# Where token rows begin in SBUF: high rows at 32, low rows at 160 modulo 256 bytes, and eight idle matmuls instead of fourteen

## The chip, the cores and the metric

The kernel runs on one core of one Trainium2 chip. The metric is the device time of one execution in microseconds (us); lower is better. Before the change it is 1536.18 us, the median of three runs that lie between 1535.31 and 1536.74 us.

## What is computed

The reference is one step of a decoder layer in which three head groups work side by side. It takes a new sequence of 4096 tokens and 64 sample tokens (8 sequences of 8), each a row of 1024 numbers:

```
h = rmsnorm(x, g_pre)
z = h @ w_in                      # 1024 -> 2816 columns
cb, cc, ch, cg, q, k, v, ag, mq, mg = split_cols(z)
out_a = silu(cg) * cb * conv3(cc * ch)            # 256 columns
out_b = silu(ag) * window_attention(q, k, v, sink)  # 512 columns, window 128
out_c = silu(mg) * attention(mq, memory)          # 256 columns, 256 memory tokens
y = concat(out_a, out_b, out_c) @ w_out
x = x + rmsnorm(y, g_post)
```

All data are float32. The outputs are the new x for all tokens and the new caches of keys, values and convolution inputs. The change concerns the product `h @ w_in`, the first and longest part of the kernel.

## The kernel before, in words

**Number format.** TensorE is fed in the type float32r. The kernel splits each operand in two: a high part, which is the number as copied into that type, and a low part, which is the rest. A product is then the sum of three matmuls: high weights with high tokens, high weights with low tokens, low weights with high tokens. `product` (lines 362 to 369, the matmul at line 368) does this for one 128-column group of weights and 260 tokens: 4 steps over the inner dimension, 3 matmuls each, 12 in all, accumulated in one PSUM bank.

**Products.** The 4160 tokens are cut into 8 blocks of 520, two halves of 260 each. The 22 groups of 128 columns of `w_in` are taken in pairs. For the blocks from the third on in phase 0, and for all blocks in phases 1 and 2, the 2 x 2 block product of a pair of column groups is made with seven products instead of eight (`PRODUCTS`, a Strassen-like scheme with sums such as S1 to S4 of the weights and T1 to T4 of the tokens). The first two blocks of phase 0 (`plain_block`) use the ordinary eight. Phases 0 and 1 treat four pairs, phase 2 three. So the loops over phase, block, product, pair, inner step and high/low issue all matmuls of line 368, in program order.

**Order of the work.** While the products of one step run, the parts for the next step are made: `split` (line 355) writes the high part with ScalarE (line 358) and the low part with VectorE (line 359); `x_split` (line 577) does the same for the first two blocks, with the gain of the norm folded in. Loading, scaling, sums, eviction of PSUM by VectorE (line 375) or ScalarE (line 377) and the finishing of each column group are issued between the products in an order written out by hand. PE takes its matmuls in that order and waits for a part only if it is late.

**Where the operands lie.** A token tile is `[128, 4, 320]` float32: per partition four rows, one for each inner step, each padded from 260 to 320 numbers. 320 numbers are 1280 bytes, five times 256, so all four rows begin at the same place modulo 256 bytes. The tiles come from the pool `hp`, two under the tag "hi" and two under "lo". A pool named `shift` with one tile of 32 numbers (128 bytes per partition) is opened just ahead of `hp` (line 92); nothing uses the tile, it only moves `hp` and every pool that is opened behind it on that side. The weight tiles are `[128, 2, 512]`, high and low, in the pools `wa` and `wb`; each weight load takes 128 numbers, 512 bytes. Weights and tokens of line 368 all begin at 224 modulo 256.

**The opening.** TensorE first runs fourteen matmuls on a tile of ones (`warm`, line 701 to 704) whose result is thrown away. Meanwhile the first tokens and weights arrive and are split; the first real product follows.

**Behind the input projection** come the attention chunks and the output projection (line 1494, 512 columns a matmul, and attention lines such as 1184, 1248, 1199 and 1271). They begin when the pools of the input projection are closed, and open pools of their own in that place. Line 791 multiplies the memory tokens by their weights, between products of phase 2.

Of the kernel before, what the change touches and what calls it, by code (L numbers as in the profile page):

```python
# [8 lines left out]
F32 = mybir.dt.float32  # L9
F32R = mybir.dt.float32r  # L10
# [5 lines left out]
P = 128  # L16
D = 1024
KT = D // P
KH = KT // 2
# [4 lines left out]
HW = 260  # L24
XR = 320
# [22 lines left out]
def f(ap):  # L48
    return ap.bitcast(F32)
# [3 lines left out]
def hybrid_layer(ctx: ExitStack, tc: tile.TileContext, a: dict):  # L53
# [31 lines left out]
    pa = ExitStack()  # L85
# [3 lines left out]

    place = ctx.enter_context(tc.tile_pool(name="place", bufs=1)).tile([P, 2, KH, HW], F32, name="place")  # L90
    hxp = pa.enter_context(tc.tile_pool(name="hx", bufs=4))
    pa.enter_context(tc.tile_pool(name="shift", bufs=1)).tile([P, 32], F32, name="shift")
    hp = pa.enter_context(tc.tile_pool(name="hp", bufs=2))
    own = ExitStack()
    kept_z = ExitStack()
# [66 lines left out]
    def store(dst, src):  # L162
        if store_queue[0] is G:
            G.dma_start(dst, src)
        else:
            late.append(lambda: DMA.dma_start(dst, src))
# [153 lines left out]
    def gain_of(o, k):  # L320
        kk = KH * (int(o[1]) - 1) + k
        return gpre[:, kk : kk + 1]
# [16 lines left out]
    def t_sum(ph, b, o):  # L339
# [9 lines left out]
        if ph == 1:  # L349
# [2 lines left out]
                tc.keep_in_program_order(ins)  # L352
            store(hd[b][o], ops[o])

    def split(src, name):
        hi = hp.tile([P, KH, XR], F32R, tag="hi", name=f"hi{name}")[:, :, :HW]
        lo = hp.tile([P, KH, XR], F32R, tag="lo", name=f"lo{name}")[:, :, :HW]
        S.copy(hi, src)
        V.tensor_tensor(lo, src, f(hi), op=ALU.subtract)
        return hi, lo  # L360
# [157 lines left out]
    def h_split(i):  # L518
        if i < len(steps):
            ph, b, p = steps[i]  # L520
            o = PRODUCTS[p][1]
            hs[i] = split(xs[ph, b][o], f"{ph}_{b}{o}")
# [52 lines left out]
    raw0, zz, pending, h0, kept = {}, {}, {}, {}, {}  # L575

    def x_split(b, o, meanwhile=lambda: None):
        x = xs[0, b][o]
        h0[b, o] = hi, lo = [hp.tile([P, KH, XR], F32R, tag=n, name=f"{n}0_{b}{o}")[:, :, :HW] for n in ("hi", "lo")]
        for k in range(KH):  # L580
            if k == 1:
                meanwhile()
            g = gain_of(o, k)
            S.mul(hi[:, k], x[:, k], g)
            V.scalar_tensor_tensor(lo[:, k], x[:, k], g, f(hi[:, k]), op0=ALU.mult, op1=ALU.subtract)
# [37 lines left out]
    def plain_jobs(b, s):  # L623

        gains = lambda b, *os: [lambda o=o: x_gain(0, b, o) for o in os]
        scales = lambda b, *os: [lambda o=o: x_scale(0, b, o) for o in os]
        parts = lambda b, o: [lambda: x_split(b, o)]
        fill = lambda o: [lambda q=q: first_fill(o, q) for q in range(4)]
        sums = lambda q, k: [lambda: first_sums(q, k)]
# [70 lines left out]
    idle = accumulator(1, 2, "idle")  # L700
    warm = hp.tile([P, KH, XR], F32R, tag="lo", name="warm").rearrange("p k n -> p (k n)")
    G.memset(f(warm[:, : P + 512]), 1.0)
    for n in (416, 416, 416, 416, 512, 512, 512, 416, 416, 416, 260, 260, 260, 260):
        TE.matmul(idle[:, 0, :n], warm[:, :P], warm[:, P : P + n], start=True, stop=True)  # L704
    x_split(0, "B11", lambda: first_fill("A21", 0))
    for q in range(4):
        if q > 0:
# [743 lines left out]
    class Block:  # L1451
# [10 lines left out]
        def split(self):  # L1462
# [13 lines left out]
            self.hl = [hi, lo]  # L1476

        def run(self, last, start, split, starts):
            b, m = self.b, self.m
            yn = work([P, D], "yn", f"yn{b}")  # L1480
# [4 lines left out]
            for p, (c0, c1) in enumerate(parts):  # L1485
                if p == 1:
                    split()
                acc = psum("z", f"y{b}_{p}")[:, : c1 - c0]
                j, passes = 0, 3 if m == P else 2
                for k in range(KT):  # L1490
                    if k in starts:
                        start()
                    for l, r in ((0, 0), (1, 0), (0, 1)) if m == P else ((0, 0), (0, 1)):
                        TE.matmul(acc, self.hl[l][:, k], wo[k][c0 // 512][:, r, c0 % 512 : c0 % 512 + c1 - c0], start=j == 0, stop=j == passes * KT - 1)  # L1494
                        j += 1
                if m < P:
                    S.copy(yn[:m, c0:c1], acc[m : 2 * m])
                    V.tensor_tensor(acc[:m], acc[:m], yn[:m, c0:c1], op=ALU.add)
                end = last and p == 2
                if not end:  # L1500
                    V.tensor_tensor(yn[:m, c0:c1], acc[:m], gpost[:m, c0:c1], op=ALU.mult)  # L1501
                S.activation((psum("t", "sq") if end else acc)[:m, : c1 - c0], acc[:m], AF.Square, scale=float(D) ** -0.5, accum_out=st[:m, p : p + 1])  # L1502
                if last and p == 1:
                    V.tensor_tensor(st[:m, 0:1], st[:m, 0:1], st[:m, 1:2], op=ALU.add)
# [180 lines left out]
```

## Time and profile before

| what | value |
|---|---|
| median of three runs | 1536.18 us |
| the profiled execution, device time | 1533.46 us |
| its span, first to last instruction | 1531.7 us |
| TensorE granted clock, mean | 0.999 |
| PE (matmul) busy | 1520.7 us, 99% of the span |
| PEld (weight load) busy | 1398.8 us, 91% |
| VectorE (DVE) busy | 1145.3 us, 75% |
| ScalarE (ACT) busy | 806.1 us, 53% |
| GpSimd (POOL) busy | 380.0 us, 25% |

The engines run side by side, so the busy times add up to more than the span. A busy row of PE or PEld counts the time from the start of an instruction to its modelled end; matmuls are pipelined, so each row overlaps the next, and the distance between two starts is shorter than the duration of one. The trace calls a token part `hi_` or `lo_` with a digit and a letter of the operand, a weight tile `w_`, the PSUM bank `c`. In a row of a group, the last figure ahead of the bar is the count, then come busy time in us and the mean duration in ns; in a row of one line's view, the three figures are the shortest, the median and the longest duration in ns, then the first and the last start. A row of a window gives its bounds in us and its length, the busy time of each engine with the number of instructions in it, the granted clock, the busy share of the DMA engines and GB/s. A row of the timeline or of the chain begins with start and length in us.

### The profile page before, as it was taken

What the parts mean: (1) busy time and instruction counts of PE and PEld (TensorE: products, weight loads), DVE (VectorE), ACT (ScalarE), POOL (GpSimd) and SP (SyncE); (2) the same over time, 40 slices, a digit from 0 to 9 for tenths busy, and PEclk for the clock granted to TensorE, in tenths of its full rate; (3) what the DMA queues carried; (4) which work ended last, traced back from release to release, by engine and by line L of the source; (5) the groups of instructions that cost most, each with busy time, mean ns of one, the idle gap of its engine ahead of it and who ended that gap; (6) DMA issues with size and microseconds to landing.
All of it is one profiled execution on the core that took longest, in us unless ns stands there. A gap on an engine that the chain in (4) does not pass through costs nothing.

```text
span 1531.7 us, 30162 instructions
## 1 busy us (share of the span) xinstructions
PE 1520.7 (99%) x11337; PEld 1398.8 (91%) x11337; DVE 1145.3 (75%) x2055; ACT 806.1 (53%) x2039; POOL 380.0 (25%) x604
## 2 busy tenths in 40 slices
PE   9999999999999999999999999999999999999998
PEld 9999999999999999999999998788888888888876
DVE  6789888898978777897777679766666666666743
ACT  6786566476222222354454447755665565565632
POOL 0223332221400000000101204544444444444310
PEclk9999999999999999999999999999999999999999
DMA  9989999878755333677877789977777777776332
GB/s 257 199 225 246 274 283 267 277 244 284 194 181 181 127 126 127 225 231 278 229 272 227 230 291 260 239 151 159 148 148 151 155 156 150 160 161 146 131 110 96
DMA packets 177942, 306.28 MB, mean 200 GB/s; under 512 B 33925, under 2 KB 107653, under 8 KB 177765
## 3 DMA queue, kind: packets, MB, share of 16 engines
q1 hardware_dynamic: 130901, 227.38, 48.2%
q0 software_dynamic: 46176, 75.92, 25.1%
q8 instruction: 90, 1.47, 0.4%
q10 hardware_dynamic: 720, 1.05, 0.2%
q14 instruction: 55, 0.45, 0.1%
HBM read 197.23 MB, written 108.05 MB: 199 GB/s over the span
## 4 chain that ended last, share of the span: by engine, by line
PE 93%; DVE 3%; DMA 1%; ACT 1%; issue 1%; POOL 0%; SPq 0%; DVEq 0%; POOLq 0%; ACTq 0%
PE c L368 53%; PE y L1494 23%; PE ws L1248 4%; PE wo L1090 2%; PE wt L1271 2%; PE xs L1184 2%; PE xt L1199 2%; PE wo L1220 2%; PE wo L1226 1%; PE mem_acc L791 1%; DMA nat<-in_x_p 1%; DMA ws18A<-in_w_in 0%; DMA ws20A<-in_w_in 0%; DVE x_2T L348 0%; PE idle L704 0%
## 5 line engine op out<-in xcount | busy, mean ns | idle before, releaser
L1494 PE MATMUL y<-wo,mh 128*128 128x512 f32 (+1 forms) x1040 | 350.1, 399 | 0.0
L375 DVE TENSOR_TENSOR z<-c,z 128x520 f32<-128x520 f32 (+1 forms) x308 | 195.0, 647 | 88.8 <-PE c L368 87.5
L1494 PEld LDWEIGHTS y<-wo,mh 128*128 128x128 f32 x1040 | 194.3, 188 | 39.3 <-issue 2.4
L1494 PE MATMUL y<-wo,ml 128*128 128x512 f32 (+1 forms) x520 | 201.8, 388 | 0.0
L1261 ACT ACTIVATE sm<-sm,wnm 128x128 f32<-128x128 f32 x256 | 99.6, 390 | 61.0 <-DVE wnm L1255 59.7
L1193 POOL TENSOR_SCALAR xp<-xp,xrd 128x256 f32<-128x256 f32 x128 | 74.6, 590 | 207.1 <-DVE xrd L1189 207.0
L1494 PEld LDWEIGHTS y<-wo,ml 128*128 128x128 f32 x520 | 98.2, 189 | 16.2
L1185 DVE TENSOR_REDUCE xmx<-xs 128x2 f32<-128x512 f32 x64 | 44.1, 689 | 59.4 <-PE xs L1184 59.3
L1273 ACT COPY wpt<-wt 128x512 f32<-128x512 f32 x64 | 37.3, 582 | 86.3 <-PE wt L1271 83.7
L1248 PEld LDWEIGHTS ws<-kst,q 128*128 128x128 f32 x512 | 70.0, 190 | 5.4 <-ACT xp L1188 0.7
L1501 DVE TENSOR_TENSOR yn<-y,gpost 128x512 f32<-128x512 f32 (+1 forms) x66 | 45.1, 684 | 39.6 <-PE y L1494 39.3
L1248 PE MATMUL ws<-kst,q 128*128 128x256 f32 x512 | 73.1, 283 | 0.4 <-ACT xp L1188 0.4
L1502 ACT ACTIVATE y<-y 128x512 f32<-128x512 f32 (+1 forms) x66 | 38.6, 585 | 64.2 <-DVE yn L1501 64.2
L739 POOL CAST wmask<-negs 128x256 uint8<-128x256 f32 x1 | 0.6, 610 | 266.4 <-DMA negs<-in_wmask 266.4
L1281 POOL TENSOR_SCALAR_AFFINE_SELECT wpt<-wpt 128x512 f32<-128x512 f32 x64 | 52.8, 824 | 42.1 <-ACT wpt L1273 39.1
L1188 ACT ACTIVATE xp<-xs,xnm 128x256 f32<-128x256 f32 x128 | 58.9, 464 | 7.1 <-DVE xnm L1186 7.1
L1123 POOL DMA_DIRECT2D q<-qd x64 | 42.8, 674 | 71.0 <-DVE wo L186 60.9
L1112 POOL DMA_DIRECT2D kst<-qd x64 | 38.6, 616 | 63.7 <-PE xt L1199 41.5
L1251 DVE COPY_PREDICATED sm<-wmask,ws 128x256 f32<-128x256 uint8 x124 | 52.2, 436 | 2.7 <-ACT sm L1250 2.5
L1512 DVE SCALAR_TENSOR_TENSOR xr<-yn,yst,xr 128x1024 f32<-128x1024 f32 (+2 forms) x34 | 43.1, 1269 | 14.0 <-POOL yst L1508 13.3
L1278 POOL TENSOR_SCALAR_AFFINE_SELECT wpv<-wpt 128x512 f32<-128x512 f32 x62 | 40.2, 648 | 50.9 <-ACT wpt L1273 50.8
L377 ACT COPY z<-c 128x520 f32<-128x520 f32 (+1 forms) x44 | 24.4, 554 | 51.9 <-PE c L368 47.9
(962 smaller groups left out, 5116.4 us busy)
## 6 DMA issues: line engine op xcount, KB each, us to landing
q<-qd POOLq DMA_DIRECT2D x64, 384.0 KB, 8.2
xr<-in_x_p SPq DMA_DIRECT2D x32, 512.0 KB
nat<-in_x_p SPq DMA_DIRECT2D x39, 416.0 KB
o_yp<-xr SPq DMA_DIRECT2D x31, 512.0 KB
md<-th POOLq DMA_DIRECT2D x48, 260.0 KB, 6.5
qd<-zh SPq DMA_DIRECT2D x48, 260.0 KB
qd<-z SPq DMA_DIRECT2D x48, 260.0 KB
kst<-qd POOLq DMA_DIRECT2D x60, 192.0 KB, 5.7
```

What stands on the lines that cost most here:

```text
L368: TE.matmul(bank[:, :HW], l, r, start=first and i == 0, stop=last and i == 3 * KH - 1)
L375: add = lambda dst, other: V.tensor_tensor(dst, c, other, op=ALU.add)
L1185: V.tensor_reduce(mx[:, :nb], s, axis=AX.X, op=ALU.max)
L1188: S.activation(p[:, i, :], s[:, i, :], AF.Exp, bias=nm[:, i : i + 1], scale=SCALE, accum_out=den[:, i : i + 1])
L1193: G.tensor_scalar(p[:, i, :], p[:, i, :], rd[:, i : i + 1], 0.5, op0=ALU.mult, op1=ALU.mult)
L1248: TE.matmul(s3[:, hh, :], self.q[:, 4 + 2 * (2 * half + hh) + kvh, i * P : i * P + P], self.kst[:, 2 * kvh + part, i * P : i * P + 2 * P], ...
L1251: V.copy_predicated(sm[:, 2 * half : 2 * half + 2, :], third["wmask"], third["negs"] if first else s3[:, :, 0:P])
L1261: S.activation(sm[:, hh, :], sm[:, hh, :], AF.Exp, bias=nm[:, hh : hh + 1], scale=SCALE, accum_out=den[:, hh : hh + 1])
L1281: G.affine_select(p3, p3, pattern=[[0, 4], [1, P]], compare_op=ALU.is_ge, fill=0.0, base=0, channel_multiplier=-1)
L1494: TE.matmul(acc, self.hl[l][:, k], wo[k][c0 // 512][:, r, c0 % 512 : c0 % 512 + c1 - c0], start=j == 0, stop=j == passes * KT - 1)
L1501: V.tensor_tensor(yn[:m, c0:c1], acc[:m], gpost[:m, c0:c1], op=ALU.mult)
L1512: V.scalar_tensor_tensor(self.xr[:m, cs], yn[:m, cs], st[:m, 3:4], self.xr[:m, cs], op0=ALU.mult, op1=ALU.add)
```

## The change

The unused pool `shift` goes. Each token tile is taken with an offset: a high tile's rows begin 48 numbers (192 bytes) behind the start of the padded row, a low tile's 16 numbers (64 bytes). The tiles themselves now begin 128 bytes lower, so high rows begin at 32 and low rows at 160 modulo 256. The weights' pool is opened earlier and keeps its place. All pools that are opened behind `hp` on the same side begin 128 bytes lower too. The last six of the fourteen idle matmuls are left out.

```
-    pa.enter_context(tc.tile_pool(name="shift", bufs=1)).tile([P, 32], F32, name="shift")
...
+    begins = {"hi": 48, "lo": 16}
+
+    def split_tile(tag, name):
+
+        n = begins[tag]
+        return hp.tile([P, KH, XR], F32R, tag=tag, name=name)[:, :, n : n + HW]
+
     def split(src, name):
-        hi = hp.tile([P, KH, XR], F32R, tag="hi", name=f"hi{name}")[:, :, :HW]
-        lo = hp.tile([P, KH, XR], F32R, tag="lo", name=f"lo{name}")[:, :, :HW]
+        hi, lo = split_tile("hi", f"hi{name}"), split_tile("lo", f"lo{name}")
...
-        h0[b, o] = hi, lo = [hp.tile([P, KH, XR], F32R, tag=n, name=f"{n}0_{b}{o}")[:, :, :HW] for n in ("hi", "lo")]
+        h0[b, o] = hi, lo = [split_tile(n, f"{n}0_{b}{o}") for n in ("hi", "lo")]
...
-    for n in (416, 416, 416, 416, 512, 512, 512, 416, 416, 416, 260, 260, 260, 260):
+    for n in (416, 416, 416, 416, 512, 512, 512, 416):
```

## The prediction, made before the change was run

> **What bounds the kernel now.** I read the page first: busy shares, clock and the chain that ended last.
>
> ```profile
> span 1531.7 us, 30162 instructions
> PE 1520.7 (99%) x11337; PEld 1398.8 (91%) x11337; DVE 1145.3 (75%) x2055; ACT 806.1 (53%) x2039; POOL 380.0 (25%) x604
> PE 93%; DVE 3%; DMA 1%; ACT 1%; issue 1%; POOL 0%; SPq 0%; DVEq 0%; POOLq 0%; ACTq 0%
> ```
>
> TensorE (PE) is busy 99% of the span and carries 93% of the chain, so what shortens or lengthens the step from one matmul to the next goes straight into the time. The change touches line 368, the products with the token parts "hi" and "lo", 53% of the chain. How fast do they follow each other? Next I read the chain in order of time, and busy time in a stretch of 100 us with line 368 alone:
>
> ```profile
> 2.16 4.37 PE idle L704 x14
> ...
> 82.84 9.36 DMA nat<-in_x_p
> ...
> 479.46 225.15 PE c L368 x1895
> ...
> 876.57 52.04 PE c L368 x432
> ```
> ```profile
> 500.00:600.00 100.00, 100.00 (x845) 100.00 (x844) 1.00 0.36 126
> ```
>
> In the 225.15 us, 1895 matmuls follow each other without a gap; less the 0.28 us by which the last one outlasts its start, that is 118.7 ns each. The second piece, 432 matmuls of the same shape, has (52.04 - 0.28) / 432 = 119.8 ns each. The window shows the full clock (1.00) and PE and its weight loader (PEld) busy all the time. So the step of line 368 is not a constant of its shape: the same 260 columns, 128 weights and addresses run at 118.7 or at 119.8 ns. That is what a pair of read streams, moving tokens and next weights, can do that get into each other's way depending on how they fall together.
>
> **Do start addresses matter?** The program before puts every token row and every weight row of line 368 at 224 modulo 256 bytes (the summary gives the 224 of the weights; the token rows follow from the diff, which lowers their tiles by 128 and adds 192 for high, 64 for low). Line 1494 has 512 columns, also 224 against 224. From its list of tile addresses, the query tiles, which are the weights of the next group of matmuls, begin at 160 in odd chunks and at 96 in even ones. So the last matmul of each group of line 1494 streams from 224 while weights from 160 or 96 are loaded. The groups of lines in short windows, first chunk 9 (160), then chunk 10 (96), then line 1494 as a whole between 940 and 1470 us (224):
>
> ```profile
> L1494 PE MATMUL y<-wo,mh 128*128 128x512 f32 x1 | 0.4, 388 | 0.0
> ```
> ```profile
> L1494 PE MATMUL y<-wo,mh 128*128 128x512 f32 x1 | 0.4, 396 | 0.0
> ```
> ```profile
> L1494 PE MATMUL y<-wo,mh x888: 387/393/499, 940.0 to 1469.8; 128*128 128x512 f32 x178
> ```
>
> 388 ns where the weights begin 64 bytes below the stream, 396 where they begin 128 below, a median of 393 (minimum 387) where both begin alike. The opposite sign, stream at 160 and next weights at 224, occurs where the memory products of line 791 hand over to line 368:
>
> ```profile
> L791 PE MATMUL mem_acc<-mparts 128*128 128x512 f32 x1 | 0.4, 388 | 0.0
> ```
>
> Also 388. These durations include a tail, but differences between them are differences of the step: the timeline below has three matmuls in 0.68 us, 227 ns each, where rows of 0.39 us stand.
>
> ```profile
> 1500.31 0.61 PE L1494 MATMUL y<-wo,mh 128*128 128x512 f32 x2
> 1500.77 0.39 PE L1494 MATMUL y<-wo,ml 128*128 128x512 f32 x1
> 1500.99 0.61 PE L1494 MATMUL y<-wo,mh 128*128 128x512 f32 x2
> ```
>
> So beside 512 columns, an offset of 64 bytes either way is worth about 4 to 5 ns against equal starts, and 128 bytes costs 3. The change gives just these offsets: high rows at 32 are 64 above 224 (modulo 256), low rows at 160 are 64 below.
>
> A Trainium skill page speaks against any effect. "TensorE: Matmul & The Clock Gate", section "Part 2: What happens when you issue a matmul", says of the two read ports: "Loading the next tile's weights doesn't steal SBUF read bandwidth from the running matmul." By that rule the sum would be no change at all; the trace disagrees, with 388 against 396 ns for one stream beside different weight addresses.
>
> For 260 columns the trace has a counter-sign. The last matmul of line 368 ahead of the memory products streams from 224 while weights at 160 are loaded, the same offset as the high rows will have. Its row stands beside a row of the stretch from 500 to 600 us:
>
> ```profile
> L368 PE MATMUL c<-hi_1T,w_2S 128*128 128x260 f32 x1 | 0.3, 283 | 0.0
> ```
> ```profile
> L368 PE MATMUL c<-hi_5T,w_0S 128*128 128x260 f32 x24 | 4.8, 281 | 0.0
> ```
>
> 283 against 281: 2 ns slower, from a single matmul whose successor has another shape too.
>
> **The change, part by part.** *Token starts.* Line 368 runs 7,488 times: 2 plain blocks x 8 products x 48, then 6 and 8 blocks x 7 products x 48, then 8 x 7 x 36. Two of three stream a high row, one a low row. Per matmul the bounds are -5 ns (388 against 393, beside 512 columns) and +2 ns (283 against 281, beside 260). I take -1.5. A weight load of 128 columns lies beside every matmul of either width, so what the two streams cost each other should go by the load; but beside 260 columns load and stream are about equally long, so a saving on one may be swallowed by the other, and the nearest row says +2. That puts me at about a third of the 512-column gain: 7,488 x -1.5 ns = -11.2 us.
>
> *What gives part of it back.* PE waits a few times for VectorE, whose chains start from PE but then run on their own. The three longest absences of PE from the chain are 82.8 to 112.5, 415 to 439 and 457 to 479 us. These 76 us end in rows such as
>
> ```profile
> 112.51 0.39 PE L368 MATMUL c<-lo_2T,w_0S 128*128 128x260 f32 x1 [0.47 <-DVE lo_2T L359]
> ```
> ```profile
> 439.03 0.39 PE L368 MATMUL c<-lo_2T,w_0S 128*128 128x260 f32 x1 [0.89 <-DVE lo_2T L359]
> ```
>
> There a 1.3% faster PE only waits longer: 76 x 1.3% = 1.0 us is lost.
>
> *Everything else that moves.* Without the 128-byte pad the tiles behind the token parts (z, the temporary tiles, the row tiles) begin 128 bytes lower. VectorE's scaling of z touches tiles with four different starts modulo 256 (224, 32, 96 and 160 in the list of tile addresses) and takes the same time on all, so I cost the move at nothing; the cover is VectorE's own slack, 15% in a stretch where PE never waits.
>
> ```profile
> L620 DVE TENSOR_TENSOR z<-z,rb x8: 1230/1234/1242, 60.4 to 109.5; 128x1040 f32<-128x1040 f32 x8
> ```
> ```profile
> 130.00:230.00 100.00, 100.00 (x845) 100.00 (x845) 84.73 (x102) 63.84 (x112) 34.31 (x52) 1.00 1.00 267
> ```
>
> The output stage opens its pools where the token pool has been closed, and its addresses stay.
>
> *Six idle matmuls less.* These are the timeline of the start, then from the idle line's own view the first eight, and the eighth with the ninth:
>
> ```profile
> 5.09 0.60 ACT L182 CAST w_0A<-wr_0A 128x512 fp32r<-128x512 f32 x1
> ...
> 6.36 0.28 PE L368 MATMUL c<-hi_0B,w_0A 128*128 128x260 f32 x1
> ...
> 10.70 0.69 DVE L186 TENSOR_TENSOR w_3A<-wr_3A,w_3A 128x512 fp32r<-128x512 f32 x1 [0.93 <-ACT w_3A L182]
> ...
> 11.44 0.51 PE L368 MATMUL c<-hi_0B,w_3A 128*128 128x260 f32 x2
> ...
> 12.74 0.28 PE L368 MATMUL c<-hi_0B,w_0A 128*128 128x260 f32 x1
> ```
> ```profile
> L704 PE MATMUL idle<-warm x8: 548/588/713, 2.2 to 5.0; 128*128 128x416 f32 x5, 128*128 128x512 f32 x3
> ```
> ```profile
> L704 PE MATMUL idle<-warm x2: 522/535/548, 5.0 to 5.3; 128*128 128x416 f32 x2
> ```
>
> The ninth starts at 5.3, so that is when PE is free after eight; the first weights are cast at 5.69, and the first product can start at about 5.75 in place of 6.36. That 0.6 us is worth nothing: the fourth weights are ready at 11.39, when VectorE ends, and the matmul that needs them starts at 11.44 as now. What could it cost? The idle ones run slow at first: eight with 5 x 416 + 3 x 512 = 3,616 columns take 3.1 us, 0.87 ns a column, where line 368 has 118.7 / 260 = 0.46. If the 0.4 us hole held that slow state, the 48 products up to 12.74 would need 48 x 260 x 0.87 ns = 10.9 us from 5.75, ending at 16.6: at most 3.9 us. I take 0, since PE has worked 3.1 us by then and real products follow at once.
>
> Sum on the profiled execution: 1533.46 us (span 1531.7) - 11.2 + 1.0 = 1523.3. The median of the runs is 1536.18, 2.7 above that execution, so the forecast as a median is 1526.0 us.
>
> **Rivals.** *No effect (1536.2).* Ports independent, or the saving swallowed whole because weight load and stream end together. For it: hi and lo rows alike sit at one step now; against it: 388 against 396. *Slower: the other rhythm.* The late piece shows that line 368 can settle at 119.8 ns and stay there; the new offsets could make that the usual rhythm, as the 283 hints. Price: 1.1 ns x (7,488 - 432) = +8 us, 1544; with the full 2 ns +15 us, 1551. It decides once the mean step rises by 0.41 ns, 3.1 us in all. *Slower by the start alone.* Addresses do nothing and TensorE stays slow in the opening: 1540.1. *Part of the gain stopped by DMA.* From 130 to 230 us the DMA share is 1.00; if transfers bind there, the 27% of matmuls in that phase (2,016) gain nothing and the result is 1529, inside my forecast's range.
>
> **How the numbers follow.** About 0.2% (3.1 us) is what a measurement can tell from no change. Forecast 0.55: its own range is 1510 (-3.5 ns each) to 1532. No effect 0.17. Other rhythm 0.23, 1540 to 1551. Start alone 0.05. So faster 0.55, same 0.17, slower 0.28. The range that leaves out 2 in 10 cuts the far ends on both sides: 1512 to 1547.
>
> **What would show it.** Right: in a gapless stretch of line 368 the count per 100 us rises from 845 to about 856, the mean durations fall below 281, and line 1494 keeps its 387/393. The slower rival would show 837 or fewer and 283. The opening is right if the first product with the fourth weights still starts at about 11.4 us; wrong if products before it stand 0.22 us apart or more. The forecast is wrong as a mechanism if the time falls while that count stays, or if high and low matmuls move in opposite ways and cancel.

## The result, and the profile after

The kernel after takes 1531.21 us, the median of 12 runs (1529.03 to 1533.39), against 1535.95 us for the kernel before in the same session (12 runs). The ratio is 0.9971, its 95% interval 0.996 to 0.9981: 4.7 us or 0.3% faster. The forecast was -10.2 us, so the direction held and the size did not. The profiled execution took 1529.03 us, 4.4 less than that of before. The page of the kernel after, span, busy times and chain by engine:

```profile
span 1527.3 us, 30150 instructions
PE 1514.2 (99%) x11331; PEld 1391.6 (91%) x11331; DVE 1145.1 (75%) x2055; ACT 806.2 (53%) x2039; POOL 381.0 (25%) x604
PE 87%; DVE 5%; issue 4%; DMA 2%; POOL 1%; ACT 1%; SPq 0%; ACTq 0%; POOLq 0%; DVEq 0%
```

PE is 6.5 us less busy (1.0 of it the idle matmuls, see below) and still fills 99%, but it now carries 87% of the chain and not 93%: the rest went to VectorE, issue and DMA. The product's line is now 373 (in kernels with further edits up to 375), line 1494 is now 1499. Two windows of the kernel after with line 373 alone, then its chain in order of time:

```profile
500.00:600.00 100.00, 100.00 (x851) 100.00 (x850) 1.00 0.38 134
130.00:230.00 100.00, 100.00 (x851) 100.00 (x850) 1.00 1.01 266
```
```profile
111.08 186.74 PE c L373 x1583
...
466.20 5.71 DMA ws20A<-in_w_in
476.94 223.46 PE c L373 x1895
...
872.05 51.17 PE c L373 x432
```

851 matmuls per 100 us in place of 845, and the same number where DMA is at 1.01 as where it is at 0.38. The piece of 1895 gives the step: (223.46 - 0.28) / 1895 = 117.77 ns, where before had 118.67. The last 432, which the prediction read as 119.8 ns before, now run at (51.17 - 0.28) / 432 = 117.8. (One start to the next, those 432 stand 120.0 ns apart in the trace of before; the piece's length underrates them a little.) (A window also counts the matmul that is still running at its left edge, so its step is 100.28 / 851 = 117.84; the chain's pieces are the finer measure.) High and low rows do not move alike. Groups of the stretch from 500 to 600 us, after:

```profile
L373 PE MATMUL c<-hi_4T,w_1S 128*128 128x260 f32 x24 | 4.7, 282 | 0.0
L373 PE MATMUL c<-lo_5T,w_1S 128*128 128x260 f32 x12 | 3.3, 278 | 0.0
```

and the low group of the same stretch before, which stood at the 281 of the high rows:

```profile
L368 PE MATMUL c<-lo_5T,w_2S 128*128 128x260 f32 x12 | 3.4, 281 | 0.0
```

Where did the rest go? 7,488 steps that are 0.89 ns shorter make 6.7 us; the last matmul ends only 4.4 us earlier. The timeline, before and then after, shows where PE now waits longer, and one place where it waits less (435.71, which the prediction shows at 439.03 with 0.89).

```profile
479.46 0.39 PE L368 MATMUL c<-lo_3T,w_0S 128*128 128x260 f32 x1 [0.28 <-DVE lo_3T L359]
...
956.09 0.60 PE L1271 MATMUL wt<-ident,sm 128*128 128x128 f32 x4
```
```profile
343.98 0.39 PE L373 MATMUL c<-lo_0B,w_0A 128*128 128x260 f32 x1 [0.71 <-DVE lo_0B L364]
...
435.71 0.39 PE L373 MATMUL c<-lo_2T,w_0S 128*128 128x260 f32 x1 [0.54 <-DVE lo_2T L364]
...
475.67 0.39 PE L373 MATMUL c<-hi_3T,w_0S 128*128 128x260 f32 x1 [0.22 <-ACT hi_3T L363]
476.94 0.39 PE L373 MATMUL c<-lo_3T,w_0S 128*128 128x260 f32 x1 [0.89 <-DVE lo_3T L364]
...
951.80 0.63 PE L1276 MATMUL wt<-ident,sm 128*128 128x128 f32 x4 [0.89 <-DVE xrd L1194]
```

VectorE (at 475.67 ScalarE) now delivers parts up to 0.9 us late that it had in time, or nearly, before: at 343.98 and about 476 us in phase 1 of the products, and at 951.80 us in the attention chunks, where PE did not wait before.

Waits are not all of it. In phase 2, groups of 36 product matmuls alternate with other work of PE. One such group in the chain before, then the same group and a later one after:

```profile
781.55 4.28 PE c L368 x36
```
```profile
777.01 4.32 PE c L373 x36
...
787.04 4.25 PE c L373 x36
```

Nine groups of the kernel after, between 771 and 862 us, take 4.32 or 4.33 us, where most of its other groups take 4.24 or 4.25; eight of the nine took 4.27 or 4.28 before. That is (4.32 - 4.25) / 36, about 2 ns a matmul more; inside these nine the starts stand 120.0 ns apart. Compared start by start, the 1,008 matmuls from 721.61 to 861.87 us gain 0.1 us in all, where 1,008 x 0.89 ns would be 0.9. So the step of 117.8 does not hold everywhere in the kernel after, as 118.7 did not hold everywhere before.

The opening of the kernel after, from the timeline:

```profile
2.15 3.38 PE L709 MATMUL idle<-warm 128*128 128x416 f32 x8 [2.15 <-POOL warm L707]
5.68 0.59 PE L373 MATMUL c<-hi_0B,w_0A 128*128 128x260 f32 x1
6.06 0.42 PE L373 MATMUL c<-lo_0B,w_0A 128*128 128x260 f32 x1
6.40 0.80 PE L373 MATMUL c<-hi_0B,w_0A 128*128 128x260 f32 x2
7.00 0.34 PE L373 MATMUL c<-lo_0B,w_0A 128*128 128x260 f32 x1
...
10.53 0.69 DVE L185 TENSOR_TENSOR w_3A<-wr_3A,w_3A 128x512 fp32r<-128x512 f32 x1 [1.04 <-ACT w_3A L181]
...
11.34 0.44 PE L373 MATMUL c<-hi_0B,w_3A 128*128 128x260 f32 x2
...
12.56 0.28 PE L373 MATMUL c<-hi_0B,w_0A 128*128 128x260 f32 x1
```

The eight idle matmuls take 3.38 us, where fourteen took 4.37. The first matmul of a product starts 0.68 us earlier than before (5.68 for 6.36), the one behind the first 48 only 0.18 us earlier (12.56 for 12.74). And the output projection between 934 and 1466 us, after, has kept its durations of 387/393/499 ns:

```profile
L1499 PE MATMUL y<-wo,mh x889: 387/393/499, 934.6 to 1465.8; 128*128 128x512 f32 x178
```

### The profile page after: what moved, and what is told of

Same layout as the page of the kernel before. It is cut to its first block, busy times and chain, and to the rows that moved or that the text cites. A ratio compares the mean times of both kernels' runs of the same rounds, so it can differ in the third digit from the quotient of the medians.

```text
span 1527.3 us, 30150 instructions
## 1 busy us (share of the span) xinstructions
PE 1514.2 (99%) x11331; PEld 1391.6 (91%) x11331; DVE 1145.1 (75%) x2055; ACT 806.2 (53%) x2039; POOL 381.0 (25%) x604
## 4 chain that ended last, share of the span: by engine, by line
PE 87%; DVE 5%; issue 4%; DMA 2%; POOL 1%; ACT 1%; SPq 0%; ACTq 0%; POOLq 0%; DVEq 0%
PE c L373 47%; PE y L1499 23%; PE ws L1253 4%; PE wo L1095 2%; PE wt L1276 2%; PE xs L1189 2%; PE xt L1204 2%; PE wo L1225 2%; PE wo L1231 1%; PE mem_acc L796 1%; DVE z L380 1%; DMA ws10A<-in_w_in 1%; DMA vd<-v 1%; DMA place<-hd_B 0%; DMA ws20A<-in_w_in 0%
## 5 line engine op out<-in xcount | busy, mean ns | idle before, releaser
L275 ACT ACTIVATE nat<-nat 104x1024 f32<-104x1024 f32 x40 | 42.3, 1057 | 18.5 <-DMA nat<-in_x_p 18.5
```

## The experiments

All kernels below are edits of the kernel after and compute the full result. "Distance" is the start of a token row less the start of the weights, modulo 256 bytes, with the sign that makes it smallest: before has 0 for high and low rows, after +64 for high and -64 for low. "Count" is the number of matmuls of the product's line from 500 to 600 us, a stretch in which PE never waits in any of them.

### The two halves of the change

`idle_only`: the token rows back at 224, eight idle matmuls. `starts_only`: the new starts, fourteen idle matmuls.

```
# idle_only
+    pa.enter_context(tc.tile_pool(name="shift", bufs=1)).tile([P, 32], F32, name="shift")
-    begins = {"hi": 48, "lo": 16}
+    begins = {"hi": 0, "lo": 0}
# starts_only
-    for n in (416, 416, 416, 416, 512, 512, 512, 416):
+    for n in (416, 416, 416, 416, 512, 512, 512, 416, 416, 416, 260, 260, 260, 260):
```

Expected, in that order:

> Only the six idle matmuls are left out; token rows stay at 224. If the opening is set by the fourth split weights, the matmul on them starts at about 11.4 us as before, the count per 100 us stays 845, and the time is that of before, 1536 us within 2. If the idle matmuls carry the gain of the change, about 1531; if the opening stays slow, 1538 to 1540.

> Only the token starts change (high 32, low 160); fourteen idle matmuls stay. If the starts carry the whole gain: 851 matmuls of the product line per 100 us as in the changed kernel, high rows 282 ns and low rows 278, time 1531 us within 2. If the idle matmuls carry it: 1536.

Measured: idle_only 1537.63 us, ratio to before 1.0011 (1.0 to 1.0023). starts_only 1529.16 us, ratio 0.9957 (0.9942 to 0.9973). The windows, idle_only, then starts_only:

```profile
500.00:600.00 100.00, 100.00 (x845) 100.00 (x844) 1.00 0.33 116
```
```profile
500.00:600.00 100.00, 100.00 (x851) 100.00 (x850) 1.00 0.37 131
```

The starts carry the whole gain. Six idle matmuls less save nothing, and may cost something: idle_only lies 1.75 us above before; `w0_equal` (below), which also has eight and distance 0 but other addresses, lies 0.13% above it (1.0013, 1.0001 to 1.0025); and the kernel after lies 2.05 us above starts_only. Each of these is at the edge of the noise, but all lean the same way; it stays open. The expectation that the matmul on the fourth weights starts at about 11.4 us did not hold in the profiled execution of idle_only, the slowest of its twelve:

```profile
11.79 0.40 PE L374 MATMUL c<-hi_0B,w_3A 128*128 128x260 f32 x2
```

### Is it each matmul's own distance?

The result's 282 and 278 invite the simplest reading (theory A): a matmul's cost goes by its own distance, +1 ns at +64, -3 ns at -64. Then low distances for all rows would be better still. The rival (B): it only matters that successive matmuls begin at different places. `swap` exchanges the offsets (high at 160, low at 32: distances -64 and +64), `both160` puts all rows at 160 (-64), `both32` all at 32 (+64).

```
-    begins = {"hi": 48, "lo": 16}
+    begins = {"hi": 16, "lo": 48}   # swap
+    begins = {"hi": 16, "lo": 16}   # both160
+    begins = {"hi": 48, "lo": 48}   # both32
```

Expected, in that order:

> High rows at 160, low rows at 32, weights 224, eight idle. Theory A (each matmul's cost goes by its own start against the next weights: 64 below saves 3 ns, 64 above costs 1 or nothing): high rows now 278 ns, low rows 282, mean step 116.8 ns, about 859 per 100 us, 1523 us. Theory B (what counts is that successive streams begin in different places, whichever they are): mean step 117.8, 851 per 100 us, 1531 us.

> High and low rows at 160, weights 224, eight idle. Theory A (own start against the next weights): all rows 278 ns, mean step 115.9, about 865 per 100 us, 1515 us. Theory B (successive streams must begin in different places): all steps like those from high to high, 118.7 to 119.2 ns, 842 to 845 per 100 us, 1536 to 1540 us.

> High and low rows at 32, weights 224. If each matmul's cost goes by its own start against the weights (theory A): all rows like the high rows now, step 118.4 to 119.2 ns, about 844 per 100 us, 1535 us. If equal starts in succession are what costs (theory B): 120 ns as with both at 160, 836 per 100 us, 1542 us. If costs of ordered pairs of starts simply add, the step from 32 to 32 comes out of the runs so far at about 111 ns, 900 per 100 us, under 1490 us.

Measured: swap 1546.91 us (1.0068, 1.0045 to 1.009), both160 1542.28 (1.0042, 1.0023 to 1.006), both32 1542.28 (1.0046, 1.0028 to 1.0063). All three are slower than before. Windows of swap and of both160, then a piece of the chain of both32:

```profile
500.00:600.00 100.00, 100.00 (x831) 100.00 (x830) 1.00 0.33 116
```
```profile
500.00:600.00 100.00, 100.00 (x836) 100.00 (x835) 1.00 0.34 118
```
```profile
482.93 227.67 PE c L373 x1895
```

both32 runs at (227.67 - 0.28) / 1895 = 120.0 ns. -64 for all rows and +64 for all rows give the same 120.0, against 118.67 with distance 0 and 117.77 with the mixed pair, so no sum over single matmuls can be made of them: theory A falls. swap has successive starts that differ exactly as in the kernel after, and is the slowest of all, 100.28 / 831 = 120.7 ns: theory B falls too. Its high and low rows, from the groups between 500 and 600 us:

```profile
L373 PE MATMUL c<-hi_4T,w_1S 128*128 128x260 f32 x24 | 4.8, 285 | 0.0
...
L373 PE MATMUL c<-lo_5T,w_1S 128*128 128x260 f32 x12 | 3.4, 280 | 0.0
```

Against 281 the high rows are longer and the low rows shorter, as after, though their distances are exchanged. What a row takes depends on its neighbours.

### Is it the distance, or the place itself?

`w96` moves the weights 128 bytes, to 96, and keeps the token rows of after (32 and 160): their distances become -64 and +64, those of swap. `all128` moves weights and tokens by 128 bytes: distances of after, at other addresses. Two pads of 128 bytes that nothing uses do it. If the tokens' own places count (theory D), w96 is like after; if the distances count (theory C), w96 is like swap and all128 like after. `both96` puts all rows at 96, distance 128.

```
# w96 and all128
+    ctx.enter_context(tc.tile_pool(name="left", bufs=1)).tile([P, 32], F32, name="left")
+    ctx.enter_context(tc.tile_pool(name="right", bufs=1, side="right")).tile([P, 32], F32, name="right")
# w96 too
-    begins = {"hi": 48, "lo": 16}
+    begins = {"hi": 16, "lo": 48}
# both96 alone, without the pads
+    begins = {"hi": 0, "lo": 0}
```

Expected, in that order:

> Token rows as in the changed kernel (high 32, low 160), but the weights at 96: a pad of 128 bytes ahead of every pool on both sides moves everything by 128, and the tokens' offsets are exchanged. Theory C (only the start relative to the weights counts): high rows are 64 below and low rows 64 above the weights, as in the kernel with the starts exchanged, so 831 matmuls per 100 us and 1547 us. Theory D (only the token rows' own starts and their succession count, the weights don't matter): as in the changed kernel, 851 per 100 us and 1531 us.

> The changed kernel with the same 128-byte pads and its own offsets: high rows at 160, low rows at 32, weights at 96, so every distance modulo 256 is that of the changed kernel. Theory C (relative starts): 851 per 100 us, 1531 us. Theory D (the token rows' own starts): as with the starts exchanged, 831 per 100 us, 1547 us.

> High and low rows at 96, 128 bytes away from the weights at 224. The 512-column matmuls took 396 ns at that distance against a median of 393 at equal starts. If the distance to the weights rules (A and C): 3 ns more than before, step about 121 ns, 828 per 100 us, 1555 us. If only succession counts (B and D): 120 ns, 836 per 100 us, 1542 us.

Measured: w96 1548.32 us (1.0086, 1.0065 to 1.0107), all128 1533.27 (0.999, 0.9974 to 1.0006), both96 1548.04 (1.0083, 1.0062 to 1.0104). Windows of w96, of all128, and of both96 (two stretches):

```profile
500.00:600.00 100.00, 100.00 (x831) 100.00 (x830) 1.00 0.33 116
```
```profile
500.00:600.00 100.00, 100.00 (x851) 100.00 (x850) 1.00 0.37 129
```
```profile
500.00:600.00 100.00, 100.00 (x828) 100.00 (x827) 1.00 0.33 116
130.00:230.00 100.00, 100.00 (x835) 100.00 (x835) 1.00 1.01 263
```

w96 has the count of swap to the matmul, and all128 that of after. Theory C stands, D falls. all128 also shows how a gained step can be lost again: with the step of after its median is no better than before's within the interval. Of the waits of its PE these two are the longest but for the one at the start; the kernel after has the same two with 0.9 and 0.7 us:

```profile
PE wt L1278 <- DVE xrd L1196: 2.2, 1, 2.2
PE idle L711 <- POOL warm L709: 2.2, 1, 2.2
PE c L375 <- DVE lo_0B L366: 1.5, 1, 1.5
```

Why these waits are longer at other addresses was not tried. A faster PE is not needed for the first of them: it is 1.2 us in idle_only, 0.7 in both32 and 1.7 in hi224_lo96 (below), none of which has the step of after, and absent in starts_only, which has.

both96 shows two rhythms, that is, steps kept over a long stretch, with one set of addresses: 835 (120.1 ns) in one stretch, 828 (121.1 ns) in the other.

The next four kernels cross the addresses by 32 bytes. Theory W is that the place of the weights within a block of 64 bytes decides (224 and 96 lie alike in it). `w0_64_192` has weights at 0 and the distances of after, `w0_equal` those of before, `w0_32_32` distance 32 for all; `both0` has weights at 224 and distance 32.

```
# the three w0 kernels
+    ctx.enter_context(tc.tile_pool(name="left", bufs=1)).tile([P, 8], F32, name="left")
+    ctx.enter_context(tc.tile_pool(name="right", bufs=1, side="right")).tile([P, 56], F32, name="right")
-    begins = {"hi": 48, "lo": 16}   # kept in w0_64_192
+    begins = {"hi": 32, "lo": 32}   # w0_equal
+    begins = {"hi": 40, "lo": 40}   # w0_32_32, and both0 without the pads
```

Expected, in that order:

> The distances of the changed kernel (high rows 64 above the weights, low rows 64 below), but everything begins 32 bytes further: weights at 0, high 64, low 192, and the operands of the later stages too. Theory C (distances alone): 851 per 100 us, 1531 us. Theory W (a weight load that begins on a 64-byte boundary touches eight blocks in place of nine, 13.3 ns less of loading): the step falls to the 109 to 116 ns that load and stream would need alone, 865 to 920 per 100 us; line 1494 may fall under 387 ns as well; 1490 to 1515 us.

> The distances of the kernel before (tokens and weights begin alike) with everything at 0 modulo 256. Theory C: 845 per 100 us, 1536 us. Theory W: 865 to 920 per 100 us, 1490 to 1515 us.

> Weights at 0, tokens at 32: the same distance of 32 as in the kernel with tokens at 0, but here it is the weights that begin on the boundary. Theory C: the same count as there. Theory W: 865 to 920 per 100 us, 1490 to 1515 us.

> Tokens at 0, weights at 224: tokens begin on a 64-byte boundary, 32 above the weights. Theory C gives it a value of its own, between those of distances 0 and 64: 836 to 845 per 100 us, 1536 to 1542 us. Theory W: no gain, as the weights still touch nine blocks: 836 to 845. If the stream's own blocks limit: as many blocks (17), so no gain either.

Measured: w0_64_192 1531.5 us (0.9984, 0.997 to 0.9998), w0_equal 1535.74 (1.0013, 1.0001 to 1.0025), w0_32_32 1542.02 (1.0055, 1.0037 to 1.0073), both0 1542.07 (1.0056, 1.004 to 1.0073). The windows in that order:

```profile
500.00:600.00 100.00, 100.00 (x851) 100.00 (x851) 1.00 0.37 134
```
```profile
500.00:600.00 100.00, 100.00 (x846) 100.00 (x845) 1.00 0.34 124
```
```profile
500.00:600.00 100.00, 100.00 (x836) 100.00 (x835) 1.00 0.33 118
```
```profile
500.00:600.00 100.00, 100.00 (x836) 100.00 (x835) 1.00 0.33 118
```

The weights' place shows no effect of its own on the count: 851 as after, 846 as before (845), and 836 twice. Theory W falls; no run shows the 13.3 ns or the 109 to 116 ns of its expectation.

### Which distances are good?

In each of four kernels either the high or the low rows keep a distance that was good (+64, -64 or 0) and the other rows do not get the one that went with it; the theories G, H and I are stated in the expectations.

```
-    begins = {"hi": 48, "lo": 16}
+    begins = {"hi": 48, "lo": 32}   # hi32_lo224: +64 and 0
+    begins = {"hi": 48, "lo": 0}    # hi32_lo96: +64 and -128
+    begins = {"hi": 32, "lo": 16}   # hi224_lo160: 0 and -64
+    begins = {"hi": 32, "lo": 0}    # hi224_lo96: 0 and -128
```

Expected, in that order:

> High rows at 32 (64 above the weights), low rows at 224 (equal to the weights). Theory G (it is enough that low rows start elsewhere than high rows): 851 per 100 us or more, 1531 us or less. Theory H (the high rows' distance decides, 64 above is the good one): also about 851, 1531. Theory I (only the pair 64 above and 64 below together is good): 836 to 845, 1536 to 1542 us.

> High rows at 32 (64 above the weights), low rows at 96 (128 away). Theories G and H: about 851 per 100 us, 1531 us. Theory I: 836 or fewer, 1542 us or more, as both distances alone gave 836 and 828.

> High rows at 224 as before the change, low rows at 160 (64 below the weights). Theory G: 851 or more, 1531 us or less. Theory H: 845 as before, 1536 us. Theory I: 836 to 845, 1536 to 1542 us.

> High rows at 224 as before the change, low rows at 96 (128 away). Theory G: 851 or more, 1531 us or less. Theory H: 845, 1536 us. Theory I: 828 to 845, 1536 to 1548 us.

Measured, in that order: 1543.24 us (1.0043, 1.0028 to 1.0058), 1543.52 (1.0053, 1.0035 to 1.0072), 1542.66 (1.0041, 1.0026 to 1.0057) and 1543.4 (1.005, 1.0031 to 1.007). Windows of hi32_lo96, then a piece of the chain of hi224_lo160:

```profile
500.00:600.00 100.00, 100.00 (x828) 100.00 (x828) 1.00 0.33 116
130.00:230.00 100.00, 100.00 (x836) 100.00 (x835) 1.00 1.01 262
```
```profile
483.70 178.72 PE c L373 x1487
```

(178.72 - 0.28) / 1487 = 120.0 ns; the other two have the same count, 836. Neither the +64 of the high rows nor the -64 of the low rows brings anything by itself, and 0 is only good when all rows have it. Of these theories only I fits, by which the gain belongs to the pair.

How narrow is the pair? Theory J: +64 and -64 stands alone. Theory K: it is enough that high rows lie above the weights and low rows below. Two kernels keep the signs and halve one distance, then both.

```
-    begins = {"hi": 48, "lo": 16}
+    begins = {"hi": 48, "lo": 24}   # hi32_lo192: +64 and -32
+    begins = {"hi": 40, "lo": 24}   # hi0_lo192: +32 and -32
```

Expected, in that order:

> High rows at 32, low rows at 192, weights at 224: distances +64 and -32 bytes; eight idle matmuls. Theory J (the fast rhythm belongs to the one pair +64 and -64; every other pair of unequal distances falls back on the 120.0 ns rhythm): 836 matmuls in the stretch from 500 to 600 us, about 1542 us. Theory K (it is enough that high rows lie above the weights and low rows below, the amount is loose): 849 to 852 matmuls, 1529 to 1533 us.

> High rows at 0, low rows at 192, weights at 224: distances +32 and -32 bytes; eight idle matmuls. Theory J (only +64 and -64): 836 matmuls in the stretch from 500 to 600 us, about 1542 us. Theory K (high above, low below, any amount): 849 to 852 matmuls, 1529 to 1533 us.

Measured: hi32_lo192 1541.5 us (1.0048, 1.0033 to 1.0062), hi0_lo192 1542.2 (1.0039, 1.0022 to 1.0055). Chain pieces of the two:

```profile
482.57 227.67 PE c L373 x1895
```
```profile
482.92 204.64 PE c L373 x1703
```

120.0 ns both, (204.64 - 0.28) / 1703 for the second: J. Altogether the step against the distances, each from a long stretch without a wait:

| distances, high and low | kernels | step, ns |
|---|---|---|
| +64, -64 | after, starts_only, all128, w0_64_192 | 117.8 |
| 0, 0 | before, idle_only, w0_equal | 118.7 |
| +64, +64; -64, -64; +32, +32 (two kernels); +64, 0; 0, -64; 0, -128; +64, -32; +32, -32 | nine kernels | 120.0 |
| 128, 128; +64, -128 | both96, hi32_lo96 | 120.0 and 121.1 |
| -64, +64 | swap, w96 | 120.7 |

So 120.0 ns is the usual step, and before and after are the exceptions. Even these fall back to it in places: the last 432 matmuls of before run at 120.0 throughout, and nine groups of after do (777.01 above). So the distances set the step of the long stretches, but in a given stretch something besides them decides too. What inside TensorE lets just these two sets of distances run below 120.0, and what makes them lose it, stays open; nothing in the trace shows the read streams themselves. No version is shown to beat the kernel after.

## Why the prediction was right and wrong, step by step

**What bounds the kernel.** Right in the main: PE stays at 99% in every kernel, and the time follows the step of the product's line, but for all128, which has the step of after and hardly any of its gain.

**Do start addresses matter?** Right that they do; the rows of 388 and 396 were a true sign of it. On the rule of the Trainium skill that the prediction weighed ("TensorE: Matmul & The Clock Gate", Part 2: a weight load does not steal read bandwidth from the running matmul): w96 and all128 share the place of the weights and differ in the token rows alone, 831 against 851, which that rule doesn't provide for. What failed is the reading "an offset of 64 bytes either way is worth about 4 to 5 ns against equal starts", carried over as a price for each matmul. Beside 260 columns an offset of 64 either way, given to all rows, costs 1.3 ns (both32 and both160: 120.0 against 118.67). By the prediction's own steps swap would have been costed like the change, at -11.2 us; it came out 11 us slower than before. The direction was therefore right by luck: it hung on the pairing of signs, which the argument did not contain.

**The term of -1.5 ns.** This is the step that was mis-sized: -0.89 ns x 7,488 = -6.7 us in place of -11.2, which is 4.5 of the 5.5 us by which the forecast missed. The two bounds, -5 and +2, held the value; the third of the 512-column gain was too much, and the nearer row, 283 against 281, kept its sign for the high rows (282).

**What gives part of it back.** Forecast 1.0 us, measured about 2.3: 6.7 less the 4.4 by which the last matmul ends earlier. These are figures of one execution of each kernel. The starts of the matmuls in the two traces, compared one by one, show where: each gapless block of 336 matmuls (phases 0 and 1) gains 0.30 us, as 336 x 0.89 ns says; the wait at 343.98 turns one block's gain into a loss of 0.6, those at 475.67 and 476.94 another's into one of 0.8. At the last product PE is 5.4 us ahead; the wait at 951.80 takes 1.06 of that. The prediction looked for the give-back where PE was absent from the chain before: of those three places one gave some back (476.94) and two did not (111.08 and 435.71). It missed two where VectorE had been in time, 343.98 and 951.80, the second of them behind the products, and the groups of phase 2 that run at 120.0 ns (0.8 us). The wait at 951.80 varies between kernels with the same step, from none in starts_only to 2.2 us in all128, and is there in slower kernels too, so its cause is open. A rival for part of the loss is the opening: the median of starts_only, with fourteen idle matmuls, is 6.7 us below before, the full 7,488 x 0.89 ns, and that of the whole change 4.7. The profiled executions of the two don't tell them apart (1529.03 us both).

**Everything else that moves.** Costed at nothing: the output projection kept 387/393/499, and between 500 and 600 us PE never waits. Right for these, and VectorE's busy time stayed as well (1145.3 and 1145.1 us); the wait at 951.80, which comes and goes between the kernels, this term left out.

**The idle matmuls.** No gain, as forecast; that they cost nothing is not shown (idle_only 1.0011, and see above). The reason given held in part: the matmul that needs the low part of the fourth weights starts at 11.34 (11.44 before), close behind VectorE's 10.53 + 0.69 = 11.22 (11.39 before). But this time PE came to it at its usual step, 0.12 us behind the matmul ahead; the lead was gone earlier. The slow state that the prediction priced at up to 3.9 us did reach over the hole, but for some of the products only: the first four take (7.00 - 5.68) / 4 = 0.33 us each, against 0.12 later. They used up the 0.6 us that PE was free earlier. The prediction's sign for a wrong opening, products 0.22 us apart or more, was thus there; in this execution it cost the lead and no more.

**The rivals.** "The other rhythm" was a true mechanism with nearly its price: forecast 1544, measured 1541.5 to 1543.4 in the nine kernels at 120.0 ns. It was wrong only for this pair, for which even the late piece fell to 117.8, and in nine groups of phase 2 it was right for this pair too. "DMA stops part of the gain" is refuted by 851 at a DMA share of 1.01. "No effect" falls with the ratio of starts_only.

**The signs named ahead.** Count: 856 forecast, 851 measured. The mean durations fell only for the low rows; "high and low matmuls move in opposite ways" was named as a sign that the mechanism is wrong. They did (282 and 278 for 281), without cancelling, and the mechanism was wrong: the steps go by the whole sequence of rows, and not by the single matmul.

## What to carry to other kernels

Where PE is busy without a gap, measure the start of the moving rows against the start of the weights modulo 256 bytes as a tuning size, for the actual sequence of matmuls and column count: of the sets of distances tried here one saved 0.1 to 0.4% against equal starts, depending on the kernel, and eleven cost 0.4 to 0.9%, which no price per matmul foretold. Before an effect seen beside one shape is multiplied by thousands of matmuls of another, test it with its mirror image: if the argument gives the same price to the exchanged signs, it has no mechanism yet. And of a gain on the bound engine, look for parts that arrive just in time, not only for those that arrive late already, and check in every stage that the new step is kept.

## What the runs showed of the hardware that was not expected

In the long stretches the step of a 260-column matmul takes a few fixed values, 117.8, 118.7, 120.0, 120.7 and 121.1 ns; moving all addresses together by 32 or 128 bytes leaves it as it is. The clock is 1.00 in all of them, and all kernels but both96 and hi32_lo96 keep their step between stretches with DMA shares of 0.33 and 1.02. The Trainium skill's "TensorE: Matmul & The Clock Gate", Part 2, section "Back-to-back issue gap", gives the columns at 2.4 GHz and about 2.5 ns for a matmul by itself, which is an estimate of 110.8 ns for 260 columns; the page says that this under-counts at small widths because it leaves out the weight load. The sequences here, each matmul with its own load, are 6 to 9% above it. One program can run at two steps: 118.7 and 120.0 before, 117.8 and 120.0 after, and 120.0 and 121.1 with all rows at distance 128 or at +64 and -128.
